# Reciprocal roots as a power on GpSimd, and late additions moved behind a row scaling

## The chip, the cores and the metric

The kernel runs on one core of a Trainium2 chip. A core has five engines that work side by side, each in the order of its own queue: TensorE (PE) multiplies matrices, VectorE (DVE) and ScalarE (ACT) do elementwise work, GpSimd (POOL) does elementwise work on SBUF alone, and SyncE (SP) issues DMAs. The metric is the device time of one execution in microseconds (us), lower is better. Before the change it is 1952.07 us, the median of 3 runs (1950.82 to 1953.63).

## The reference

One layer of a streaming encoder on 1024 tokens with 1024 features, float32: a feed-forward part, an attention, and another feed-forward part, each behind a root-mean-square norm.

```python
def rms_norm(x, gain):
    y = xf * lax.rsqrt(jnp.mean(xf * xf, axis=-1, keepdims=True) + NORM_EPS)
    return y * gain

x = x + 0.5 * swiglu(rms_norm(x, n1), wi1, wo1)      # 1024 -> 2 x 2816 -> 1024
x = x + stick_breaking_attention(rms_norm(x, mix_norm), w_qkv, q_gain, k_gain, w_o)
x = x + 0.5 * swiglu(rms_norm(x, n2), wi2, wo2)
```

In the attention there are 16 heads of 64 features. q and k of every token and head go through the same norm over their 64 features. With z = q k / 8 the weight of an earlier token s for token t is sigmoid(z[t,s]) times the product of sigmoid(-z[t,j]) over the tokens j between them; the output is the weighted sum of v, times w_o.

## The kernel before, in words

Tokens are kept in 8 blocks of 128 rows, in the order 4, 5, 6, 7, 0, 1, 2, 3 (ORDER). Every product is made of three float32r products of high and low parts (mm3, L275): a value is split into a rounded copy made by ScalarE and the rest made by VectorE or GpSimd (split, L183).

The feed-forward parts work with seven half-size products instead of eight. In ffn_out (L509) these are run in the order of SEVEN: 5, 1, 4, 3, 7, 2, 6. Each adds its four banks of PSUM, named ma or mb, to one or two quarters of x (result, L570, the additions are L573 on VectorE). For all but one product this follows at once. Product 2 is the exception: its banks, mb, are read later, during product 6, which works in ma. finish_late (L536) makes these late additions in two parts, and LATE (L88) says for each part behind which operand chunk of product 6 its additions are issued (the low part of that chunk on VectorE) and for which of the four row blocks: part 0 behind chunk 2 for blocks 0 and 1, part 1 behind chunk 4 for blocks 2 and 3. Each block takes two additions, since product 2 goes to two quarters. Part 0 is called ahead of chunk 0's products, part 1 behind them.

The norm in front of the attention is woven into the end of that first feed-forward part, by the function named at (L666), which ffn_out calls at given points. Rows 4 and 5 are normed when product 7 is done. For rows 6 and 7, squares and roots (rates, L223) are made during product 2 and the scaling (L245) during product 6, behind chunk 4's low part; they are transposed (turned, L252, the transposes are L257) into the four mb banks at product 6's first block. Rows 0 to 3 get their squares in two halves, ScalarE's L221; the second half and the rest of the norm follow each block's result. Row 0 is transposed at product 6's last block, the others among the first matmuls of the attention, where row 3's norm is also made.

rsqrt (L189) is the reciprocal root: a scaling to the mean plus epsilon (a), a first guess from the bits of the number (L198), and three Newton steps of three VectorE instructions each (L200 to L202). For a norm of rows it starts from sums added on VectorE (L230) and all is on VectorE. For q and k the a is made by ScalarE (L197), and y lies in a free corner (room) of the PSUM bank that the projection used.

The attention works head pair by head pair, eight pairs. For each, qkv (L750) projects the 8 row blocks to q, k, v in two halves of four blocks, half 1 first, in PSUM banks bq. finish (L771) empties a bank: squares, copies of q and k and v's high part on ScalarE (L774, L775, L778), v's low part (L779) and the sums of squares (L780) on VectorE. After the fourth block of a half it makes the root of 128x16 sums of squares, copies k's part of it to r (L786), multiplies k's rows by r on GpSimd (L790, L793) and puts q's part times 0.125 and -0.125 into f (L797), which scales the sigmoids (L856). Scores (L852) are followed per tile by two sigmoids on ScalarE (L856), a running product as a scan on VectorE (L858) and a product on GpSimd (L865, behind a memset, L863); these weights are transposed by TensorE (L887), split (th on ScalarE, tl on VectorE, L185 and L186) and multiplied with v (L905, bank bo).

What runs when is laid out in a plan: each pair has four parts a, b, c, d with lengths, the steps of all functions get due times in them, and they are issued in the order of these times; each engine's own queue is then ordered at build time by priority and expected readiness, which issue_after constrains. Pair p + 1's projections are spread over pair p, so that one root falls in part c and one in d or a.

Weights of a pair come in four pieces by DMA and are split by ScalarE (L742) and GpSimd (L745). weights_of (L720) can hold a split back: it writes a small instruction (L740) into the tile that the split will write, whose input is some other value, so that the split can't start before that value is there. For the pairs after the second, the first two pieces are held by r on VectorE (for the high part) and by k's product on GpSimd (for the low part). For the first pair, the last two pieces are held by the transposed row 7 (last_x, on GpSimd), and the first two by nothing.

After the first feed-forward part x goes to DRAM (L673) in SP's queue; the stores of rows 0 to 3 are kept in a list, stores, and issued behind the first pair's weight loads.

Of the kernel before, what the change touches and what calls it, by code (L numbers as in the profile page):

```python
# [17 lines left out]
P = 128  # L18
T = 1024
D = 1024  # L20
# [64 lines left out]

ON_POOL_H = {2: (1,), 6: (1, 3, 5)}

LATE = ((2, (0, 1)), (4, (2, 3)))  # L88

W_OF = {  # L90
    1: ((0, 0), (1, 1), "add"), 2: ((0, 0),), 3: ((0, 1), (1, 1), "subtract"), 4: ((1, 0), (0, 0), "subtract"),
# [17 lines left out]
def macaron_kernel(ctx, tc, x, g1, w1_in, w1_out, gm, w_qkv, gq, gk, w_o, g2, w2_in, w2_out, out):  # L109
# [64 lines left out]
    make_identity(nc, ident)  # L174
    xh = cpool.tile([P, KD, T], F32R, name="xh")
    xl = cpool.tile([P, KD, T], F32R, name="xl")
    above = cpool.tile([P, 104], F32, name="above")
    pool_e.memset(below, 0.0)
    pool_e.memset(above, 0.0)
    x_keep = [dram.tile([T, D], F32, name=f"x_keep{i}") for i in range(2)]  # L180
    o_keep = [dram.tile([NP * P, T], F32, name=f"o_keep{n}") for n in "hl"]

# [3 lines left out]
            (engine or dve).tensor_tensor(lo, raw, hi.bitcast(F32), op=ALU.subtract).ins,  # L186
        )

    def rsqrt(pool, ss, inv_n, y=None):  # L189

        shape = list(ss.shape)
        a, u = (pool.tile(shape, F32, name=f"rs_{n}", bufs=2 if y is None else 1) for n in "au")
        if y is None:
            y = pool.tile(shape, F32, name="rs_y")
            dve.tensor_scalar(a, ss, inv_n, EPS, op0=ALU.mult, op1=ALU.add)
        else:
            act.activation(a, ss, AF.Copy, scale=inv_n, bias=EPS)  # L197
        dve.tensor_scalar(y.bitcast(I32), a.bitcast(I32), -0.5, -550020641.0, op0=ALU.mult, op1=ALU.add)  # L198
        for _ in range(3):
            dve.scalar_tensor_tensor(out=u, in0=y, scalar=0.5, in1=a, op0=ALU.mult, op1=ALU.mult)  # L200
            dve.tensor_tensor(u, u, y, op=ALU.mult)
            dve.scalar_tensor_tensor(out=y, in0=u, scalar=1.5, in1=y, op0=ALU.subtract, op1=ALU.mult)  # L202
        return y

    def load_gain(pl, g):
# [14 lines left out]
                junk = pl["hs"].tile([P, NHALF], F32, name="hs", bufs=1)  # L220
                act.activation(junk, row(tb, h), AF.Square, accum_out=ss[:, i, h : h + 1])  # L221

    def rates(pl, row, tbs, ss=None):  # L223

        n = len(tbs)
        if ss is None:
            ss = pl["xs"].tile([P, n, 2], F32, name="ss")
            squares(pl, row, tbs, ss)
        st = pl["xs"].tile([P, n], F32, name="st")
        dve.tensor_tensor(st, ss[:, :, 0], ss[:, :, 1], op=ALU.add)  # L230
        return rsqrt(pl["xs"], st, 1.0 / D)

    def norm(pl, row, tbs, gain, ss=None, r=None, behind=None):

        if r is None:
            r = rates(pl, row, tbs, ss)
        turns = []  # L240
        for i, tb in enumerate(tbs):
            xs = pl["xs"].tile([P, D], F32, name="xs")
            with tc.issue_after(behind) if behind is not None else nullcontext():
                for h in range(2):
                    dve.scalar_tensor_tensor(  # L245
                        out=xs[:, HALVES[h]], in0=row(tb, h), scalar=r[:, i : i + 1], in1=gain[:, HALVES[h]],
                        op0=ALU.mult, op1=ALU.mult,
                    )
            turns.append(partial(turned, xs, tb))
        return turns  # L250
# [258 lines left out]
    def ffn_out(pl, w_out, keep, x_from, ahead, at):  # L509
# [37 lines left out]
        for m, tag, fresh, goes in SEVEN:  # L547
            last = m == SEVEN[-1][0]
            late = m == SEVEN[-2][0]
            if fresh:  # L550
                open_banks[tag] = [bank(tag) for _ in range(4)]
            bs = open_banks[tag]
            ops = [operands(m, c) for c in range(len(CHUNKS))]
            for (th, h), _ in goes:
                if (th, h) not in loaded:
                    load(th, h)
                    loaded.add((th, h))

            def add(ts, cs):
                for c in cs:  # L560
                    (wh, wl), (hh, hl), _ = ops[c]
                    for i, q in enumerate(CHUNKS[c]):
                        for t in ts:
                            s = slice(t * P, (t + 1) * P)
                            mm3(
                                bs[t], [((hh[:, i, s], hl[:, i, s]), (wh[:, i], wl[:, i]))],
                                fresh and q == 0, q == NQ - 1, not fresh,
                            )

            def result(t, bs=bs, goes=goes):  # L570
                for (th, h), sign in goes:
                    xc = x_sb[h][:, 4 * (1 - th) + t, :]
                    dve.scalar_tensor_tensor(out=xc, in0=bs[t], scalar=0.5 * sign, in1=xc, op0=ALU.mult, op1=ALU.add)  # L573

            if last:
                late_result(ops, 0)
            n = len(CHUNKS) - BY_BLOCK if last else len(CHUNKS)
            for c in range(n):
                add(range(4), [c])
                at(x_sb, m, c, ops)  # L580
                if last and c == 0:
                    late_result(ops, 1)
            for t in range(4):
                add([t], range(n, len(CHUNKS)))
                if not late:
# [33 lines left out]
    with pools(*RAWS) as pr:  # L619
# [41 lines left out]
        with banks("ps2"), pools(*SECOND) as pl:  # L661
            lay_banks()
            gain_m = load_gain(pn, gm)
            half = pn["xs"].tile([P, 4, 2], F32, name="half", bufs=1)

            def at(x_sb, m, where, ops):  # L666
                def row(tb, h):
                    return x_sb[h][:, tb, :]

                def store(tbs, hs):  # L670
                    for tb in tbs:
                        for h in hs:
                            sp.dma_start(x_keep[0][rows(tb), HALVES[h]], row(tb, h))  # L673

                def turn_rows(bk, n):
                    for _ in range(n):
                        pending.pop(0)(bk)

                if (m, where) == (7, "end"):
                    pending.extend(norm(pn, row, (4, 5), gain_m))  # L680
                    store((4, 5, 6, 7), (0, 1))
                elif (m, where) == (2, 2):
                    turn_rows("ma", 2)
                elif (m, where) == (2, 3):
                    late.append(rates(pn, row, (6, 7)))
                elif (m, where) == (6, 0):

                    pending.extend(norm(pn, row, (6, 7), gain_m, r=late.pop(), behind=ops[4][2][3]))
                elif m == 2 and str(where).startswith("end"):
                    ts = slice(*((0, 2), (2, 4))[int(where[-1])])  # L690
                    squares(pn, row, range(4)[ts], half[:, ts], (0,))
                elif m == 6 and str(where).startswith("block"):
                    t = int(where[-1])
                    turn_rows("mb", (2, 0, 0, 1)[t])
                    squares(pn, row, (t,), half[:, t : t + 1], (1,))
                    last_norm = lambda: pending.extend(norm(pn, row, (t,), gain_m, half[:, t : t + 1]))
                    if t < 3:
                        last_norm()
                    else:
                        late.append(last_norm)  # L700
                    stores.append(partial(store, (t,), (0, 1)))

            ffn_out(pl | pr, w1_out, keep, x, ops, at)

# [5 lines left out]
    with ExitStack() as stack:  # L710
# [39 lines left out]
        def qkv(p, state):  # L750
# [8 lines left out]
            def step(half, i, ks):  # L759
                if i == 0 and ks.start == 0:  # L760
                    start(half)
                if ks.start == 0:
                    state["ps"] = bank("bq")
                room, ps = state["ps"][:, 3 * P :], state["ps"][:, : 3 * P]
                wh, wl = state["wq"]
                t = rows(half * 4 + i)
                mm3(ps, [((xh[:, k, t], xl[:, k, t]), (wh[k], wl[k])) for k in ks], ks.start == 0, ks.stop == KD)
                if ks.stop == KD:
                    finish(half, i, ps, room)

            def finish(half, i, ps, room):  # L771
# [8 lines left out]
                dve.tensor_reduce(out=ssq[:, i, :], in_=sq, axis=AX.X, op=ALU.add)  # L780
                if i < 3:
                    return
                y = rsqrt(pl["sq"], ssq.rearrange("p a b -> p (a b)"), 1.0 / DH, room[:, :16])
                y = y.rearrange("p (a b) -> p a b", b=4)
                r = state["r"] = pl["sq"].tile([P, 4, 4], F32, name="r", bufs=1)
                dve.tensor_scalar(r[:, :, 0:2], y[:, :, 2:4], 1.0, None, op0=ALU.mult)  # L786
# [7 lines left out]

                f = state["f", half] = pl["sq"].tile([P, 2, 4, 2], F32, name=f"f{half}")
                for n, c in enumerate((0.125, -0.125)):
                    dve.tensor_scalar(f[:, n], y[:, :, 0:2], c, None, op0=ALU.mult)  # L797

            return [
                partial(step, half, i, ks)  # L800
# [138 lines left out]
        steps = qkv(0, states[0])  # L939

        last_x = ((pool_e, 0, lambda: xl[:, KD - 1, T - P : T - P + 1].bitcast(F32)),)
        for f in weights_of(0, states[0], ((), last_x)):
            f()
        with tc.issue_after(states[0]["loaded"]):
            for f in stores:
# [212 lines left out]
```

## Time and profile before

| | |
|---|---|
| median of 3 runs | 1952.07 us (1950.82 to 1953.63) |
| the profiled execution, its own time | 1951.8 us |
| its span, first to last instruction | 1950.0 us |
| granted TensorE clock, mean | 0.999 |
| TensorE busy | 1910.0 us, 98% |
| VectorE busy | 1267.2 us, 65% |
| GpSimd busy | 1092.4 us, 56% |
| ScalarE busy | 986.9 us, 51% |
| first feed-forward part | from 0 to about 672 us |
| attention, with its output projection | to about 1316 us |

How to read the lines below. A group gives line, engine, operation, output and inputs with their shape and count, then busy time and mean length of one in ns, then the idle time of the engine just before it and what ended that. A wait line gives who waited for whom, and then the total, the count and the longest wait in us. A timeline line gives start and length in us, then the instruction; the brackets at its end tell how long the engine had been idle before it and what it waited for. Several instructions of one kind in a row are merged, xN, and the length is then that of all. A window line gives the window, its length, and the busy time of PE, PEld, DVE, ACT and POOL with their counts, the granted clock, the DMA share and GB/s.

### The profile page before, as it was taken

To read this page: it belongs to the slowest core of one execution; us is meant where nothing else is said; L and a number is where in the kernel's file an instruction comes from. 1 tells how busy PE (TensorE), PEld (TensorE's weight loads), DVE (VectorE), ACT (ScalarE), POOL (GpSimd) and SP (SyncE) were. 2 spreads that over 40 slices of the span, in tenths; PEclk is the share of its full clock that TensorE was granted. 3 is DMA by queue.
4 is the path that set the end of the run, shared out by engine and by line. 5 is a ranking of instruction groups with operands and counts; after the bars stand their busy time and mean duration, and the time that the engine had idled before them with its cause. 6 is when DMAs were issued, how large, how long until landed. Compare 5 with 4: busy or idle time off the path is not lost.

```text
span 1950.0 us, 27326 instructions
## 1 busy us (share of the span) xinstructions
PE 1910.0 (98%) x9656; PEld 1639.0 (84%) x9656; DVE 1267.2 (65%) x1834; ACT 986.9 (51%) x1802; POOL 1092.4 (56%) x963
## 2 busy tenths in 40 slices
PE   7999999999999999999999999999999999999998
PEld 7978888888888898888989897789888888888887
DVE  7855545635876867878787878475645545548644
ACT  6533443344334457777787877344433343343332
POOL 3667667655545636656655664113666666655554
PEclk9999999999999999999999999999999999999999
DMA  6223223338896411011011134521323232369973
GB/s 211 82 92 125 98 97 104 118 114 277 322 344 229 139 34 43 32 43 49 28 39 45 60 114 167 179 70 43 129 87 121 98 103 88 129 211 339 337 267 134
DMA packets 168505, 260.26 MB, mean 133 GB/s; under 512 B 11568, under 2 KB 81200, under 8 KB 168368
## 3 DMA queue, kind: packets, MB, share of 16 engines
q1 hardware_dynamic: 168368, 258.52, 38.8%
q8 instruction: 75, 1.23, 0.3%
q14 instruction: 62, 0.51, 0.1%
HBM read 198.18 MB, written 60.29 MB: 133 GB/s over the span
## 4 chain that ended last, share of the span: by engine, by line
PE 85%; DVE 8%; ACT 3%; issue 2%; POOL 2%; DMA 1%; DVEq 0%; POOLq 0%; ACTq 0%
PE ka L282 6%; PE ka L284 6%; PE ka L283 6%; PE kc L284 4%; PE kc L282 4%; PE kc L283 4%; PE kb L284 4%; PE kb L282 4%; PE kb L283 4%; PE ma L283 4%; PE ma L284 4%; PE ma L282 4%; PE bq L282 4%; PE bq L283 4%; PE bq L284 4%; PE bo L905 3%
## 5 line engine op out<-in xcount | busy, mean ns | idle before, releaser
L186 POOL TENSOR_TENSOR u<-sf,u 128x512 fp32r<-128x512 f32 x160 | 226.1, 1415 | 150.9 <-ACT u L185 147.0
L186 POOL TENSOR_TENSOR rp<-raw,rp 128x1024 fp32r<-128x1024 f32 x84 | 208.9, 2491 | 179.1 <-ACT rp L185 168.3
L186 POOL TENSOR_TENSOR u<-raw,u 128x512 fp32r<-128x512 f32 x136 | 196.2, 1448 | 164.2 <-ACT u L185 162.9
L185 ACT ACTIVATE u<-sf 128x512 fp32r<-128x512 f32 x160 | 100.7, 630 | 214.8 <-PE kb L283 86.8
L865 POOL TENSOR_TENSOR w<-w,om 128x512 f32<-128x512 f32 (+4 forms) x128 | 141.1, 1106 | 114.6 <-DVE om L858 88.3
L401 DVE TENSOR_TENSOR h<-h 128x512 f32<-128x512 f32 x110 | 135.4, 1234 | 85.9 <-POOL h L505 85.1
L282 PE MATMUL bq<-wqh,xh 128*128 128x384 f32 x512 | 174.8, 341 | 2.1 <-DVE vst L779 2.1
L284 PE MATMUL bq<-wqh,xl 128*128 128x384 f32 x512 | 172.2, 336 | 0.0
L283 PE MATMUL bq<-wql,xh 128*128 128x384 f32 x512 | 172.1, 336 | 0.0
L185 ACT ACTIVATE rp<-rh 128x1024 fp32r<-128x1024 f32 (+1 forms) x78 | 76.4, 984 | 188.0 <-issue 57.5
L282 PE MATMUL ka<-xh,u 128*128 128x512 f32 (+1 forms) x448 | 162.2, 362 | 1.5 <-ACT s L453 1.5
L283 PE MATMUL ka<-xl,u 128*128 128x512 f32 (+1 forms) x448 | 162.1, 362 | 0.0
L284 PE MATMUL ka<-xh,u 128*128 128x512 f32 (+1 forms) x448 | 161.9, 361 | 0.0
L527 DVE TENSOR_TENSOR raw<-raw 128x1024 f32<-128x1024 f32 (+1 forms) x60 | 97.6, 1629 | 99.0 <-DMA raw<-w_out 89.1
L185 ACT ACTIVATE u<-raw 128x512 fp32r<-128x512 f32 x136 | 84.9, 631 | 148.9 <-PE ka L283 101.2
L282 PE MATMUL ma<-rp 128*128 128x512 f32 x352 | 137.5, 390 | 0.0
L283 PE MATMUL ma<-rp 128*128 128x512 f32 x352 | 137.2, 390 | 0.0
L284 PE MATMUL ma<-rp 128*128 128x512 f32 x352 | 137.2, 390 | 0.0
L856 ACT ACTIVATE w<-bz,f 128x512 f32<-128x512 f32 (+2 forms) x192 | 112.5, 586 | 41.5 <-PE bz L852 38.9
L505 POOL TENSOR_TENSOR h<-h,g 128x512 f32<-128x512 f32 x80 | 113.0, 1412 | 35.1 <-DVE h L457 33.3
L430 DVE TENSOR_TENSOR sf<-raw 128x512 f32<-128x512 f32 x80 | 81.2, 1015 | 78.0 <-POOL u L186 77.9
L186 DVE TENSOR_TENSOR rp<-rh,rp 128x1024 fp32r<-128x1024 f32 (+1 forms) x70 | 106.2, 1535 | 22.6 <-ACT rp L185 19.7
(272 smaller groups left out, 5557.8 us busy)
## 6 DMA issues: line engine op xcount, KB each, us to landing
raw<-w_out SPq DMA_DIRECT2D x120, 512.0 KB, 5.4
raw<-w_in SPq DMA_DIRECT2D x88, 512.0 KB, 3.6
k<-h SPq DMA_DIRECT2D x154, 256.0 KB, 2.1
rh<-k SPq DMA_DIRECT2D x64, 512.0 KB, 5.8
raw_qkv<-w_qkv SPq DMA_DIRECT2D x64, 192.0 KB, 2.9
x_keep<-x SPq DMA_DIRECT2D x32, 256.0 KB, 3.7
x<-x_keep SPq DMA_DIRECT2D x32, 256.0 KB, 5.2
raw<-w_out SPq DMA_DIRECT2D x24, 256.0 KB, 4.7
```

The lines of the kernel that those rows point to most:

```text
L185: act.activation(hi, raw, AF.Copy).ins,
L186: (engine or dve).tensor_tensor(lo, raw, hi.bitcast(F32), op=ALU.subtract).ins,
L282: pe.matmul(dst, ah, bh, start=start and i == 0, stop=False, skip_group_check=onto)
L283: pe.matmul(dst, ah, bl, start=False, stop=False, skip_group_check=onto)
L284: pe.matmul(dst, al, bh, start=False, stop=stop and i == n - 1, skip_group_check=onto)
L401: dve.tensor_tensor(src, hb[of[0]], hb[of[1]], op=getattr(ALU, of[2]))
L430: dve.tensor_tensor(f[n], x, y, op=op)
L505: pool_e.tensor_tensor(h, h, gs[k], op=ALU.mult)
L527: dve.tensor_tensor(w[0], w[0], w[1], op=getattr(ALU, W_OF[m][2]))
L856: act.activation(to, z, AF.Sigmoid, scale=state["f", half][:, sign, tb % 4, hd : hd + 1])
L865: pool_e.tensor_tensor(wt[:, c1 : c0 + n], wt[:, c1 : c0 + n], om[:, c1 - 1 : c0 + n - 1], op=ALU.mult)
L905: pe.matmul(ot[:, :n], vv, t[:, c : c + n], start=start, stop=stop)
```

## The change

- The constant tile power holds -0.5 in each partition (a memset on GpSimd); the tile above shrinks from 104 to 96 columns.
- A new function root makes the reciprocal root in two GpSimd instructions: the scaling to a, and a to the power -0.5 as a tensor_tensor with power spread over the columns.
- In the attention, finish uses root in place of rsqrt. r is no longer a copy but a view of y, which has two buffers. The two f are made on GpSimd. Nothing of the root is on VectorE or ScalarE any more, and none of it in PSUM.
- The norm in front of the attention, with pooled=True, adds its two sums of squares on GpSimd and uses root. The other two norms keep rsqrt on VectorE.
- Both parts of the late additions are issued behind chunk 4 of product 6; they are called behind chunk 0 and chunk 1, so behind the call that scales rows 6 and 7.
- The first pair's first two weight pieces get a holding instruction on GpSimd, in the low part's tile, that reads row block 0 of x's first half, which late addition makes. For this the stores carry row along.

```diff
-LATE = ((2, (0, 1)), (4, (2, 3)))
+LATE = ((4, (0, 1)), (4, (2, 3)))
...
+    power = cpool.tile([P, 1], F32, name="power")
...
+    pool_e.memset(power, -0.5)
...
+    def root(pool, ss, inv_n, bufs):
+
+        n = ss.shape[-1]
+        a, y = (pool.tile([P, n], F32, name=f"rs_{i}", bufs=b) for i, b in zip("ay", bufs))
+        pool_e.tensor_scalar(a, ss, inv_n, EPS, op0=ALU.mult, op1=ALU.add)
+        pool_e.tensor_tensor(y, a, power.to_broadcast([P, n]), op=ALU.pow)
+        return y
...
-        dve.tensor_tensor(st, ss[:, :, 0], ss[:, :, 1], op=ALU.add)
-        return rsqrt(pl["xs"], st, 1.0 / D)
+        (pool_e if pooled else dve).tensor_tensor(st, ss[:, :, 0], ss[:, :, 1], op=ALU.add)
+        return root(pl["xs"], st, 1.0 / D, (4, 2)) if pooled else rsqrt(pl["xs"], st, 1.0 / D)
...
-            if last:
-                late_result(ops, 0)
             n = len(CHUNKS) - BY_BLOCK if last else len(CHUNKS)
             for c in range(n):
                 add(range(4), [c])
                 at(x_sb, m, c, ops)
-                if last and c == 0:
-                    late_result(ops, 1)
+                if last and c < 2:
+                    late_result(ops, c)
...
-                y = rsqrt(pl["sq"], ssq.rearrange("p a b -> p (a b)"), 1.0 / DH, room[:, :16])
-                y = y.rearrange("p (a b) -> p a b", b=4)
-                r = state["r"] = pl["sq"].tile([P, 4, 4], F32, name="r", bufs=1)
-                dve.tensor_scalar(r[:, :, 0:2], y[:, :, 2:4], 1.0, None, op0=ALU.mult)
+                y = root(pl["sq"], ssq.rearrange("p a b -> p (a b)"), 1.0 / DH, (1, 2)).rearrange("p (a b) -> p a b", b=4)
+                r = state["r"] = y[:, :, 2:4]
...
-                    dve.tensor_scalar(f[:, n], y[:, :, 0:2], c, None, op0=ALU.mult)
+                    pool_e.tensor_scalar(f[:, n], y[:, :, 0:2], c, None, op0=ALU.mult)
...
-        for f in weights_of(0, states[0], ((), last_x)):
+        added = ((pool_e, 1, lambda: stores[0].args[0](0, 0)[:, 0:1]),)
+        for f in weights_of(0, states[0], (added, last_x)):
```

The calls norm(pn, ...) and rates(pn, ...) of the norm in front of the attention get pooled=True.

More of the change, by code (lines that the diff above doesn't have):

```diff
@@ L176, in macaron_kernel @@
     xl = cpool.tile([P, KD, T], F32R, name="xl")
-    above = cpool.tile([P, 104], F32, name="above")
+    above = cpool.tile([P, 96], F32, name="above")
+    power = cpool.tile([P, 1], F32, name="power")
     pool_e.memset(below, 0.0)
     pool_e.memset(above, 0.0)
+    pool_e.memset(power, -0.5)
     x_keep = [dram.tile([T, D], F32, name=f"x_keep{i}") for i in range(2)]
@@ L187, in split, with rsqrt @@
         )
[L189 to L197, printed above, removed]
+    def rsqrt(pool, ss, inv_n):
+        a, u, y = (pool.tile(list(ss.shape), F32, name=f"rs_{n}") for n in "auy")
+        dve.tensor_scalar(a, ss, inv_n, EPS, op0=ALU.mult, op1=ALU.add)
         dve.tensor_scalar(y.bitcast(I32), a.bitcast(I32), -0.5, -550020641.0, op0=ALU.mult, op1=ALU.add)
@@ L221, in squares, with rates @@
                 act.activation(junk, row(tb, h), AF.Square, accum_out=ss[:, i, h : h + 1])
-    def rates(pl, row, tbs, ss=None):
+    def rates(pl, row, tbs, ss=None, pooled=False):
         n = len(tbs)
@@ L229, in rates, with norm @@
         st = pl["xs"].tile([P, n], F32, name="st")
-        dve.tensor_tensor(st, ss[:, :, 0], ss[:, :, 1], op=ALU.add)
-        return rsqrt(pl["xs"], st, 1.0 / D)
-    def norm(pl, row, tbs, gain, ss=None, r=None, behind=None):
+        (pool_e if pooled else dve).tensor_tensor(st, ss[:, :, 0], ss[:, :, 1], op=ALU.add)
+        return root(pl["xs"], st, 1.0 / D, (4, 2)) if pooled else rsqrt(pl["xs"], st, 1.0 / D)
+    def norm(pl, row, tbs, gain, ss=None, r=None, behind=None, pooled=False):
         if r is None:
-            r = rates(pl, row, tbs, ss)
+            r = rates(pl, row, tbs, ss, pooled)
         turns = []
@@ L668, in row, with store @@
                     return x_sb[h][:, tb, :]
-                def store(tbs, hs):
+                def store(row, tbs, hs):
                     for tb in tbs:
@@ L679, in at @@
                 if (m, where) == (7, "end"):
-                    pending.extend(norm(pn, row, (4, 5), gain_m))
-                    store((4, 5, 6, 7), (0, 1))
+                    pending.extend(norm(pn, row, (4, 5), gain_m, pooled=True))
+                    store(row, (4, 5, 6, 7), (0, 1))
                 elif (m, where) == (2, 2):
@@ L684, in at @@
                 elif (m, where) == (2, 3):
-                    late.append(rates(pn, row, (6, 7)))
+                    late.append(rates(pn, row, (6, 7), pooled=True))
                 elif (m, where) == (6, 0):
@@ L695, in at @@
                     squares(pn, row, (t,), half[:, t : t + 1], (1,))
-                    last_norm = lambda: pending.extend(norm(pn, row, (t,), gain_m, half[:, t : t + 1]))
+                    last_norm = lambda: pending.extend(norm(pn, row, (t,), gain_m, half[:, t : t + 1], pooled=True))
                     if t < 3:
@@ L700, in at @@
                         late.append(last_norm)
-                    stores.append(partial(store, (t,), (0, 1)))
+                    stores.append(partial(store, row, (t,), (0, 1)))
             ffn_out(pl | pr, w1_out, keep, x, ops, at)
@@ L763, in step @@
                     state["ps"] = bank("bq")
-                room, ps = state["ps"][:, 3 * P :], state["ps"][:, : 3 * P]
+                ps = state["ps"][:, : 3 * P]
                 wh, wl = state["wq"]
@@ L768, in step, with finish @@
                 if ks.stop == KD:
-                    finish(half, i, ps, room)
-            def finish(half, i, ps, room):
+                    finish(half, i, ps)
+            def finish(half, i, ps):
                 qk, ssq, vst = state["qk", half], state["ssq"], state["v"]
```

## Prediction

> **What bounds the kernel now.** I read the page's busy times first, then the list of TensorE's waits, then the groups by line, and last the timeline engine by engine at the two places the change touches.
>
> ```profile
> span 1950.0 us, 27326 instructions
> ...
> PE 1910.0 (98%) x9656; PEld 1639.0 (84%) x9656; DVE 1267.2 (65%) x1834; ACT 986.9 (51%) x1802; POOL 1092.4 (56%) x963
> ```
>
> TensorE is busy for 1910.0 of 1950.0 us, and the change leaves it the same matmuls. So it can give back only what lies in TensorE's waits; VectorE's busy time is no measure. The waits, with total, count and longest:
>
> ```profile
> PE kb L257 <- DVE xs L245: 11.8, 4, 9.4
> PE bo L905 <- DVE tl L186: 7.5, 15, 0.9
> PE bt L887 <- POOL w L863: 4.6, 8, 0.6
> PE mb L257 <- DVE x L573: 2.2, 2, 1.9
> PE bq L282 <- DVE vst L779: 2.1, 1, 2.1
> ...
> PE bz L852 <- DVE w L858: 1.4, 7, 0.4
> ...
> PE bz L852 <- DVE rs_u L201: 0.4, 1, 0.4
> PE bz L810 <- POOL qk L790: 0.4, 1, 0.4
> ```
>
> The first (11.8) is the first layer's norm, which the change does not touch. The mb and bq waits lie between the first feed-forward part and the attention, the others in the attention. Within reach are then 7.5 + 2.2 + 2.1 + 1.4 + 0.4 + 0.4 = 14 us at most, 0.7% of the span. The bt wait (4.6) hangs on a sigmoid, scan, product chain without any root in it; it stays. One head pair in the steady state shows the same picture, here as busy times of PE, PEld, DVE, ACT, POOL:
>
> ```profile
> 806.00:872.00 66.00, 64.07 (x387) 58.86 (x385) 52.82 (x102) 51.52 (x112) 37.97 (x57) 1.00 0.13 41
> ```
>
> TensorE has 1.9 us idle in 66; GpSimd has 28 us free, VectorE 13.
>
> **The change part by part.** *The attention's root* (16 times, two per pair).
>
> ```profile
> L202 DVE SCALAR_TENSOR_TENSOR bq<-rs_u,bq 128x16 f32<-128x16 f32 x48 | 8.4, 176 | 1.2
> L200 DVE SCALAR_TENSOR_TENSOR rs_u<-bq,rs_a 128x16 f32<-128x16 f32 x48 | 8.1, 168 | 1.1
> L201 DVE TENSOR_TENSOR rs_u<-rs_u,bq 128x16 f32<-128x16 f32 x48 | 7.5, 157 | 0.6
> ...
> L740 DVE TENSOR_TENSOR wqh<-r 128x2 fp32r<-128x2 f32 x12 | 5.5, 500 | 0.0
> ...
> L797 DVE TENSOR_SCALAR f<-bq 128x8 f32<-128x8 f32 x32 | 3.7, 155 | 0.2 <-issue 0.2
> L198 DVE TENSOR_SCALAR bq<-rs_a 128x16 int32<-128x16 int32 x16 | 2.7, 168 | 0.3 <-ACT rs_a L197 0.3
> L786 DVE TENSOR_SCALAR r<-bq 128x8 f32<-128x8 f32 x16 | 2.6, 163 | 0.4
> ```
>
> Out of VectorE's queue go, per root, 168 + 3 x (168 + 157 + 176) = 1.67 us of steps, 0.16 for r and 0.31 for the two f: 2.1 us, 34 in all, and one small ScalarE instruction. GpSimd gets four instructions: the scaling a, the power y, two f. Its price per instruction follows from two sizes of one line:
>
> ```profile
> L865 POOL TENSOR_TENSOR w<-w,om 128x255 f32<-128x255 f32 x16 | 11.8, 740 | 1.1 <-DVE om L858 1.1
> ...
> L865 POOL TENSOR_TENSOR w<-w,om 128x127 f32<-128x127 f32 x16 | 7.4, 465 | 1.1 <-DVE om L858 0.3
> ```
>
> (740 - 465) / 128 = 2.15 ns a column over 0.19 us fixed: 0.23 us for a (16 columns), 0.2 for each f. No row shows a power. Its floor is 0.23, one ordinary pass. A ceiling is nine ordinary passes, each with its fixed cost, as many as the steps it replaces: 9 x 0.23 = 2.1. I take one fixed cost and nine passes of columns, 0.19 + 9 x 16 x 0.00215 = 0.5 us, since it is one instruction. Then a root occupies GpSimd for 0.23 + 0.5 + 0.4 = 1.1 us, 18 us in all. Does GpSimd have room where they fall? Around one root:
>
> ```profile
> 812.57 0.41 DVE L780 TENSOR_REDUCE ssq<-sq 128x4 f32<-128x256 f32 x1
> ...
> 818.24 0.15 DVE L201 TENSOR_TENSOR rs_u<-rs_u,bq 128x16 f32<-128x16 f32 x1
> ...
> 818.86 0.93 DVE L740 TENSOR_TENSOR wqh<-r 128x2 fp32r<-128x2 f32 x2
> 819.71 0.68 DVE L186 TENSOR_TENSOR tl<-bt,th 128x512 fp32r<-128x512 f32 x1
> ```
> ```profile
> 815.28 1.01 POOL L865 TENSOR_TENSOR w<-w,om 128x383 f32<-128x383 f32 x1 [1.37 <-DVE rs_u L201]
> 818.40 1.29 POOL L865 TENSOR_TENSOR w<-w,om 128x512 f32<-128x512 f32 x1 [2.11 <-DVE rs_u L201]
> ...
> 848.98 1.30 POOL L865 TENSOR_TENSOR w<-w 128x511 f32<-128x511 f32 x1 [1.73 <-DVE rs_u L201]
> ...
> 851.65 1.05 POOL L790 TENSOR_TENSOR qk<-qk,r 128x512 f32<-128x512 f32 x1 [1.34 <-DVE r L786]
> ```
>
> The sums of squares are ready at 813.0, and GpSimd idles 1.37 + 2.11 = 3.48 us before its product of 818.40; the pair's second root has 1.73 + 1.34. So a root of 1.1 us is hidden by this idle time, and the cover ends at a power of 3.48 - 0.23 - 0.4 = 2.85 us. r comes earlier: today its first reader, L740, starts 5.9 us after the reduction; 0.73 us on GpSimd, before or behind its product of 815.28, makes that 2 to 4.
>
> Against moving it speaks GpSimd's own rate: its 1.29 us at 818.40 are for 128x512, which VectorE's tl of 819.71 does in 0.68. The Trainium skill, GPSIMD Engine Reference, section When to use GPSIMD, puts it as a rule: ordinary elementwise work belongs on VectorE, GpSimd being about 2x slower for two inputs. These two rows agree; no run here shows it for a power. By the rule the sum would be that of the last rival below, not mine.
>
> What it gives back: at 818.24 VectorE still does L201, L202, r and two f, then the two copies of r into the weights' tile (L740), 0.93 us together although ones as small take 0.16 (L201), because GpSimd's product of 818.40 runs. Only then comes the tl of 819.71 on which TensorE waits. The same wait stands in six pairs, first and last:
>
> ```profile
> 754.43 0.50 PE L905 MATMUL bo<-tl,vst 128*128 128x512 f32 x1 [0.72 <-DVE tl L186]
> ...
> 1084.90 0.50 PE L905 MATMUL bo<-tl,vst 128*128 128x512 f32 x1 [0.73 <-DVE tl L186]
> ```
>
> Six of these are 4.4 us. All goes if r is early enough that L740 passes before GpSimd's product; nothing if L740 stays beside it. I take 2.7. The nine smaller bo waits (7.5 - 4.4 = 3.1) and the seven bz waits behind w (1.4) are 4.5 together. Some follow a root that fills VectorE's queue, some a scan that came late from ScalarE: I take half, 2.2 (0 to 2.9). The two of 0.4, in the last pair, name the steps and the products behind r themselves: 0.8.
>
> New waits: L740 on VectorE now waits for GpSimd; behind it are the tl and the scans, and TensorE for them. The new GpSimd instructions also hold up VectorE's instructions that read SBUF twice, up to 0.5 us each. I charge 1.0 (0 to 3).
>
> *The norm's root and the order in front of the attention.*
>
> ```profile
> 618.83 2.74 DVE L245 SCALAR_TENSOR_TENSOR xs<-x,rs_y,gain 128x512 f32<-128x512 f32 x4
> ...
> 651.14 6.02 DVE L245 SCALAR_TENSOR_TENSOR xs<-x,rs_y,gain 128x512 f32<-128x512 f32 x4
> 657.08 2.47 DVE L573 SCALAR_TENSOR_TENSOR x<-mb,x 128x512 f32<-128x512 f32 x4
> ...
> 683.51 0.28 DVE L779 TENSOR_TENSOR vst<-bq,vst 128x128 fp32r<-128x128 f32 x1
> ```
> ```profile
> 652.45 5.57 POOL L745 TENSOR_TENSOR wql<-raw_qkv,wqh 128x384 fp32r<-128x384 f32 x4
> ...
> 677.46 1.69 POOL L740 TENSOR_TENSOR wqh<-qk 128x2 fp32r<-128x2 f32 x4 [9.51 <-ACT qk L775]
> ```
> ```profile
> 658.41 0.92 PE L257 MATMUL mb<-ident,xs 128*128 128x128 f32 x4 [1.90 <-DVE x L573]
> ...
> 683.84 0.45 PE L282 MATMUL bq<-wqh,xh 128*128 128x384 f32 x1 [2.11 <-DVE vst L779]
> ```
> ```profile
> 677.26 0.28 ACT L778 ACTIVATE vst<-bq 128x128 fp32r<-128x128 f32 x1
> ```
>
> ScalarE has evacuated its part of the bank at 677.5, but VectorE reaches its L779 only at 683.51, behind the roots of rows 2 and 3: TensorE waits 2.11. With these roots on GpSimd, which idles 9.51 us up to 677.46, VectorE is free in time: -2.1. VectorE's scaling now waits for GpSimd's power, with L573 and L779 queued behind it; the 9.51 us cover that.
>
> Scaling rows 6 and 7 takes 6.02 us beside GpSimd's weight split of 652.45 where four such instructions took 2.74 without it. The new GpSimd instruction that reads row 0 keeps the split behind the first late addition. So the scaling ends 0 to 3.28 us earlier; but now all eight late additions (2 x 2.47) stand behind it instead of four, and the transposes need the banks they free. VectorE's sum of work is the same, so the last bank comes free up to 3.28 us earlier and the wait of 2.2 shrinks by 0 to 2.2: I take -1.1, and +0.5 as the bad end for the first transposes, whose banks are free today. Queued behind the waiting GpSimd instruction are the splits and row 0's root; TensorE wants those weights only after the last block of the feed-forward part. No DMA moves on SP's queue: the stores only carry their row with them. The tiles' sizes and the one memset cost nothing: they lie at the start, beside the loads.
>
> Sum: -2.1 - 1.1 - 2.7 - 2.2 - 0.8 + 1.0 = -7.9 us. The profiled execution took 1951.8 us, 1.8 around its span, and the median of the runs is 1952.1, 0.3 more. 1951.8 - 7.9 = 1943.9, or 1944.2 as a median. All good ends together: -2.1 - 2.2 - 4.4 - 2.9 - 0.8 = -12.4, 1939.7.
>
> **The rivals.** *The waits only change their name.* L740 still meets GpSimd's product, and the small waits are scans that come from ScalarE anyway. Then only the stage before the attention gives, -3.2: 1948.9. For it: L740's mean of 0.50. Against it: r comes 2 to 4 us sooner.
>
> *Slower: the power is dear.* GpSimd works in order; past 2.85 us of power every product behind it is late, and the transposes behind that. At 4 us: 14 roots in the seven steady pairs x 1.15 = 16.1, less 3.2: +12.9, 1965. For it: no row shows a power. Against it: two times the nine-pass ceiling would be needed.
>
> *GpSimd needs twice VectorE's time for the root as well*, as it does for the product of 1.29 against 0.68. Twice 1.67 is 3.3 us of power, 0.45 past the cover, at each of 14 roots: 14 x 0.45 - 3.2 = +3.1, 1955.2. Against it: the power is one instruction, and most of the 1.67 us are the fixed cost of ten. The Trainium skill's rule above would give this.
>
> **How the numbers follow.** Forecast 0.55 (own range 1940 to 1948), names only 0.20, dear power 0.15, twice 0.10. Range 1940 to 1956: it leaves out the dear power and the tails. A measurement of this kernel tells about 0.2%, 3.9 us. Faster by more: 0.60, nearly all of the forecast and some of the second. Same: 0.22, most of the second and of the last. Slower: 0.18.
>
> **What would show it.** A power on GpSimd under 2.85 us; no 2.1 us wait at the bq bank; rows 6 and 7 scaled in 3 to 4 us; the 0.73 waits at bo mostly gone, the bt waits of 0.6 still there. It is wrong if GpSimd's power appears as the releaser of VectorE's waits, or if pairs still take 66 us.

## The result and the profile after

The changed kernel takes 1969.17 us (median of 5 runs, 1968.21 to 1973.42), beside 1952.07 (1950.82 to 1953.63) before: a ratio of 1.0092, 95% interval 1.0077 to 1.0107. It is 17 us slower where 8 us faster were forecast. The profiled execution of after is the longest of its five, 1973.42 us with a span of 1971.6, so sums made against it are some 4 us larger than those of the medians.

The page of after, its span and its busy times (the columns as before):

```profile
span 1971.6 us, 27141 instructions
...
PE 1916.4 (97%) x9656; PEld 1643.6 (83%) x9656; DVE 1233.9 (63%) x1554; ACT 983.6 (50%) x1786; POOL 1158.2 (59%) x1048
```

VectorE's busy time fell by 33.3 us. That it comes near the forecast's 34 is chance: the 34 was for the attention's root, and with the attention alone changed (a run below) it falls by 18.5. GpSimd's rose by 65.8, and by 56.3 with the attention alone, where 18 were forecast for the attention. The groups of GpSimd say why. These are the roots' two instructions and the two f:

```profile
L207 POOL TENSOR_TENSOR rs_y<-rs_a,power 128x16 f32<-128x16 f32 x16 | 46.8, 2924 | 1.2
...
L798 POOL TENSOR_SCALAR f<-rs_y 128x8 f32<-128x8 f32 x32 | 7.0, 237 | 0.0
...
L206 POOL TENSOR_SCALAR rs_a<-ssq 128x16 f32<-128x16 f32 x16 | 3.3, 204 | 5.2 <-DVE ssq L783 3.5 <-PE bt L262 1.0
...
L207 POOL TENSOR_TENSOR rs_y<-rs_a,power 128x1 f32<-128x1 f32 x4 | 2.2, 546 | 0.3
```

The scaling (0.20) and f (0.24) cost what an ordinary pass costs. The power takes 2.92 us for 16 columns and 0.55 for one: (2924 - 546) / 15 = 159 ns a column, over 0.39 us fixed. It is an expensive operation for each value, not one ordinary pass. TensorE's waits in after:

```profile
PE bt L888 <- POOL w L864: 17.9, 16, 3.8
PE kb L262 <- DVE xs L250: 11.2, 4, 9.1
PE bo L906 <- ACT th L187: 9.1, 6, 1.5
PE bo L906 <- DVE tl L188: 4.5, 14, 0.9
...
PE mb L262 <- DVE x L578: 1.1, 2, 0.5
```

The bq wait of 2.1 is gone and mb lost 1.1. But bt has grown from 4.6 to 17.9, and a wait of 9.1 for ScalarE's th is new. All rows of the two lists make 50.9 against 34.3 us, 16.6 more; TensorE's busy time is 6.4 more for the same matmuls. Together 23.0, about the 21.6 by which the span grew.

**The new wait of 1.52 us at bo**, once in each of six pairs. GpSimd, VectorE, ScalarE and TensorE around one of them, in the timeline of after:

```profile
885.76 0.20 POOL L206 TENSOR_SCALAR rs_a<-ssq 128x16 f32<-128x16 f32 x1
886.05 2.92 POOL L207 TENSOR_TENSOR rs_y<-rs_a,power 128x16 f32<-128x16 f32 x1
```
```profile
885.92 0.95 DVE L859 TENSOR_TENSOR_SCAN om<-bz,first 128x384 f32<-128x384 f32 x1
889.01 1.11 DVE L743 TENSOR_TENSOR wqh<-rs_y 128x2 fp32r<-128x2 f32 x2 [2.14 <-POOL rs_y L207]
890.57 0.69 DVE L188 TENSOR_TENSOR tl<-bt,th 128x512 fp32r<-128x512 f32 x1 [0.45 <-ACT th L187]
```
```profile
889.20 0.84 ACT L745 ACTIVATE wqh<-raw_qkv 128x768 fp32r<-128x768 f32 x1 [3.81 <-DVE wqh L743]
889.95 0.58 ACT L187 ACTIVATE th<-bt 128x512 fp32r<-128x512 f32 x1
```
```profile
890.59 0.50 PE L906 MATMUL bo<-th,vst 128*128 128x512 f32 x1 [1.52 <-ACT th L187]
```

Read it from the end. TensorE waits for th. th stands in ScalarE's queue behind the split L745 of the weights of a pair that comes two later. That split is held by VectorE's L743, which waits for y, and y is the power. ScalarE idles for 3.81 us with th behind the waiting instruction. So a holding instruction that carries nothing urgent puts the power into the path.

**The bt waits.** The second root of the pair, on GpSimd, with the scan whose product comes late, and the transposition that waits:

```profile
850.15 2.92 POOL L207 TENSOR_TENSOR rs_y<-rs_a,power 128x16 f32<-128x16 f32 x1
853.16 1.05 POOL L791 TENSOR_TENSOR qk<-qk,rs_y 128x512 f32<-128x512 f32 x1
854.18 0.44 POOL L798 TENSOR_SCALAR f<-rs_y 128x8 f32<-128x8 f32 x2
854.61 1.32 POOL L794 TENSOR_TENSOR qk<-qk,rs_y 128x256 f32<-128x256 f32 x2
855.89 0.90 POOL L866 TENSOR_TENSOR w<-w 128x127 f32<-128x127 f32 x1
```
```profile
850.67 0.42 DVE L859 TENSOR_TENSOR_SCAN w<-bz,first 128x128 f32<-128x128 f32 x1
```
```profile
856.85 0.33 PE L888 MATMUL bt<-ident,w 128*128 128x128 f32 x1 [1.05 <-POOL w L864]
```

The scan is done at 851.1, its product starts at 855.89, 4.8 us later: the power, k's products and f stand between in GpSimd's queue. The list names L864, a small memset, as releaser; by the timeline it is the queue behind the power. A wait of 1.05 to 1.07 us stands there in five pairs, one of 0.60 in a sixth. In the first and the last pair this wait is 3.81 and 3.47 us, and TensorE's clock falls behind it. The windows behind the first (the third figure from the end is the granted clock):

```profile
716.00:720.00 4.00, 1.93 (x7) 1.41 (x8) 0.00 (x0) 0.53 (x1) 3.92 (x10) 0.61 0.00 0
720.00:724.00 4.00, 4.00 (x17) 3.81 (x16) 3.34 (x5) 3.26 (x9) 1.97 (x4) 0.54 0.00 0
```

In these 8 us the clock is little more than half. The wait of 3.81 agrees with the Trainium skill, TensorE: Matmul & The Clock Gate, Part 1, by which an idle window of about 3.4 us takes the clock to half and about as long a busy one restores it. But the clock fell behind shorter waits as well: behind the last of the six waits of 1.5 named above, at 1094.98 (0.83 over 1090 to 1100), and in the profiled execution of before behind the mb wait of 1.90 (0.87 and 0.79 over 655 to 665). In the run below with the attention alone the same mb wait left it at 1.00. So no length of wait at which the clock falls comes out of these traces.

### The profile page after: what moved, and what is told of

It reads as the page before. It is cut to its first block, busy times and chain, and to the rows that moved or that the text cites. A ratio compares the mean times of both kernels' runs of the same rounds, so it can differ in the third digit from the quotient of the medians.

```text
span 1971.6 us, 27141 instructions
## 1 busy us (share of the span) xinstructions
PE 1916.4 (97%) x9656; PEld 1643.6 (83%) x9656; DVE 1233.9 (63%) x1554; ACT 983.6 (50%) x1786; POOL 1158.2 (59%) x1048
## 4 chain that ended last, share of the span: by engine, by line
PE 84%; POOL 5%; DVE 5%; ACT 4%; issue 2%; DMA 1%; SPq 0%; ACTq 0%; DVEq 0%; POOLq 0%
PE ka L287 6%; PE ka L288 6%; PE ka L289 6%; PE kc L288 4%; PE kc L287 4%; PE kc L289 4%; PE kb L288 4%; PE kb L287 4%; PE kb L289 4%; PE bq L288 4%; PE bq L287 4%; PE bq L289 4%; PE ma L289 3%; PE ma L288 3%; PE ma L287 3%; PE mb L289 3%
## 5 line engine op out<-in xcount | busy, mean ns | idle before, releaser
L532 DVE TENSOR_TENSOR raw<-raw 128x1024 f32<-128x1024 f32 (+1 forms) x60 | 89.7, 1498 | 102.7 <-DMA raw<-w_out 86.4
L857 ACT ACTIVATE w<-bz,f 128x512 f32<-128x512 f32 (+1 forms) x192 | 112.4, 586 | 44.1 <-PE bz L853 41.6
L188 DVE TENSOR_TENSOR rp<-rh,rp 128x1024 fp32r<-128x1024 f32 (+1 forms) x70 | 117.4, 1694 | 22.6 <-ACT rp L187 19.9
```

Source lines behind the costliest of these rows:

```text
L532: dve.tensor_tensor(w[0], w[0], w[1], op=getattr(ALU, W_OF[m][2]))
L857: act.activation(to, z, AF.Sigmoid, scale=state["f", half][:, sign, tb % 4, hd : hd + 1])
```

## The experiments

The theory after reading these traces: the whole loss is the power's length on GpSimd, by two ways, the products behind it in GpSimd's queue (bt) and the hold that reads r (bo). The rivals: the new order of the queues loses the time, whatever the power takes; the loss comes from the part in front of the attention; the hold has no share in it.

**The same queues, a cheap instruction in the power's place.** It computes something else: the rates are a times -0.5 instead of a to the power -0.5.

```diff
-        pool_e.tensor_tensor(y, a, power.to_broadcast([P, n]), op=ALU.pow)
+        pool_e.tensor_tensor(y, a, power.to_broadcast([P, n]), op=ALU.mult)
```

> The power is replaced by a product with the same operands (so the rates are wrong), and every engine's queue stays as it is. Theory A, the power's length: with 0.2 us in place of 2.92 the waits of 1.5 at bo and 1.05 at bt go, and the time falls to what the prediction had without this term, 1942 to 1948 us. Rival B, the place: VectorE and ScalarE now stand behind GpSimd, which makes the products with r before the attention's own products whatever the power takes; then 2.4 us of products per root stay in the way and the time stays above 1958 us.

Measured: 1946.21 us, ratio 0.9973 (0.9961 to 0.9985). Its waits, and the place where before waited 0.73:

```profile
PE bt L888 <- POOL w L864: 6.6, 10, 1.1
PE bo L906 <- DVE tl L188: 5.4, 15, 1.3
```
```profile
748.97 0.50 PE L906 MATMUL bo<-tl,vst 128*128 128x512 f32 x1 [0.22 <-DVE tl L188]
```

Every engine has its instructions in the same order as in after, only the one instruction is short, and 23 us are gone:

```profile
L207 POOL TENSOR_TENSOR rs_y<-rs_a,power 128x16 f32<-128x16 f32 x16 | 3.5, 216 | 1.2
```

The length of the power is the cause; the rival of the queues' order falls. With a cheap power the change would give 5 us (1951.24 for before beside this run).

**The norm in front of the attention alone** (the attention's root and f back on VectorE) and **the attention alone** (everything in front of it as before).

```diff
...
-                y = root(pl["sq"], ssq.rearrange("p a b -> p (a b)"), 1.0 / DH, (1, 2)).rearrange("p (a b) -> p a b", b=4)
-                r = state["r"] = y[:, :, 2:4]
+                y = rsqrt(pl["sq"], ssq.rearrange("p a b -> p (a b)"), 1.0 / DH, room[:, :16])
+                y = y.rearrange("p (a b) -> p a b", b=4)
+                r = state["r"] = pl["sq"].tile([P, 4, 4], F32, name="r", bufs=1)
+                dve.tensor_scalar(r[:, :, 0:2], y[:, :, 2:4], 1.0, None, op0=ALU.mult)
...
```

> The norm in front of the attention, the late additions and the hold by row 0 as in the changed kernel, the attention's root back on VectorE. Theory A: the norm's part gives the 4.5 us by which the fourth sum of squares came earlier (692.9 to 688.4), and the attention costs nothing: 1946 to 1949 us. Rival C, the norm's part only moves the wait into the first pair: 1951 to 1953 us.

```diff
-LATE = ((4, (0, 1)), (4, (2, 3)))
+LATE = ((2, (0, 1)), (4, (2, 3)))
...
-        return root(pl["xs"], st, 1.0 / D, (4, 2)) if pooled else rsqrt(pl["xs"], st, 1.0 / D)
+        return rsqrt(pl["xs"], st, 1.0 / D)
...
-        for f in weights_of(0, states[0], (added, last_x)):
+        for f in weights_of(0, states[0], ((), last_x)):
```

> The attention's root on GpSimd, all ahead of it as before the change. Theory A: all of the loss and none of the gain, 17 + 4.5 us over the kernel before: 1971 to 1976 us. Rival C: 1968 to 1971 us.

Measured: 1946.32 (ratio 0.9973, 0.9963 to 0.9983) and 1972.11 (1.0103, 1.0088 to 1.0118). The waits of the second:

```profile
PE bt L890 <- POOL w L866: 18.0, 16, 3.8
PE bo L908 <- ACT th L187: 9.1, 6, 1.5
...
PE bq L287 <- DVE vst L784: 2.4, 1, 2.4
```

The part in front of the attention gains 5 us and the attention's part loses about 21. The bt and bo waits of after are all there, and the bq wait has stayed with the norm's roots on VectorE.

**What of the part in front carries its gain.** The kernel with the norm alone, and in it the late additions and the first pair's weights back to the order of before: only the norm's roots lie on GpSimd.

```diff
-LATE = ((4, (0, 1)), (4, (2, 3)))
+LATE = ((2, (0, 1)), (4, (2, 3)))
...
-        for f in weights_of(0, states[0], (added, last_x)):
+        for f in weights_of(0, states[0], ((), last_x)):
```

> Of the norm's part only the roots on GpSimd; the late additions and the first pair's weight split as before the change. Theory A: the wait of 2.1 us at the bq bank goes, the waits of 2.2 at mb and the lower clock behind them (0.87 and 0.79 over 10 us) stay: 1948 to 1950 us. Rival: the roots alone carry all of the gain: 1946 to 1947 us.

Measured: 1946.51 (0.9975, 0.9965 to 0.9985), the same time as with the new order. The list of waits has no bq and still `mb`:

```profile
PE mb L267 <- DVE x L583: 2.2, 2, 1.7
```

So the roots carry the gain alone. The new order shortens the mb wait (2.2 here, 1.1 in after), and no run shows a gain in time from it.

**No hold by r.** The first way out of the bo wait, by leaving that hold out:

```diff
-                    ((dve, 0, lambda s=nxt: s["r"][:, 0, 0:1]), (pool_e, 1, lambda s=nxt: s["qk", 1][:, 0, 4, 0:1])),
+                    ((pool_e, 1, lambda s=nxt: s["qk", 1][:, 0, 4, 0:1]),),
```

> The changed kernel without VectorE's small instruction that reads r and holds back the weight split; the hold by k's product on GpSimd stays. Theory D: in part c the loss goes over this instruction (VectorE idle 2.14 us before it, ScalarE's split and th behind it), six pairs by some 1.7 us: 1957 to 1962 us. Rival E: GpSimd's own queue holds the pair anyway, since the product of 383 columns follows the root and its products: 1966 to 1970 us.

Measured: 1978.25 (1.0135, 1.0118 to 1.0152), slower still, and outside what either side expected. Nothing now keeps the split behind its place, and the queues came out in another order. ScalarE and TensorE:

```profile
782.09 0.84 ACT L745 ACTIVATE wqh<-raw_qkv 128x768 fp32r<-128x768 f32 x1 [1.06 <-DMA raw_qkv<-w_qkv]
```
```profile
784.08 0.45 PE L906 MATMUL bo<-th,vst 128*128 128x384 f32 x1 [3.00 <-ACT th L187]
```

The splits stand ahead of their DMA, and th behind them. The run says what the hold is for, and nothing on what it costs when y is late.

**The hold by another value.** v's low part of the last block of the first half is made on VectorE shortly before the root, and doesn't come from GpSimd; all queues keep the order of after.

```diff
-                    ((dve, 0, lambda s=nxt: s["r"][:, 0, 0:1]), (pool_e, 1, lambda s=nxt: s["qk", 1][:, 0, 4, 0:1])),
+                    ((dve, 0, lambda s=nxt: s["v"][:, 7, 1, 0:1].bitcast(F32)), (pool_e, 1, lambda s=nxt: s["qk", 1][:, 0, 4, 0:1])),
```

> The changed kernel, every engine's queue in the same order; VectorE's small instruction in front of the weight split reads v's last block, which VectorE itself has written, and no longer r. Theory D: in part c the loss goes over this instruction, six pairs by 1.5 to 1.75 us: 1958 to 1961 us. Rival E: GpSimd's own queue (the product of 383 columns behind the root and its products) makes TensorE wait as long at the next transposes: 1966 to 1970 us.

Measured: 1955.92 (1.0019, 1.0010 to 1.0029). Its waits, and the hold on VectorE:

```profile
PE bt L888 <- POOL w L864: 17.9, 16, 3.8
...
PE bo L906 <- DVE tl L188: 3.0, 8, 0.9
```
```profile
815.46 0.21 DVE L743 TENSOR_TENSOR wqh<-vst 128x2 fp32r<-128x2 f32 x2
```

The th wait is gone, the bt wait has not moved: two separate ways. One value that a small instruction reads is worth 1969.2 - 1955.9 = 13.3 us by the medians, and 12.3 when each is taken against before in its own runs (1952.07 and 1951.14). That is more than the six waits of 1.52 (9.1); the rest is smaller waits behind tl (4.5 to 3.0) and TensorE's busy time (1908.3 us here, 1916.4 in after). The two profiled executions differ by more, 19.1, as the one of after was the longest of its five and TensorE's clock was lower in it more often. The two instructions of the hold now take 0.21 instead of 1.11 us: beside them GpSimd is in its power (2.92 us from 814.73), and no longer in a product.

**The root in two halves**, eight columns behind two blocks each, so that half of it is done early.

```diff
...
+                if i % 2 == 0:
+                    return
+                cols = slice(8 * (i // 2), 8 * (i // 2) + 8)
+                ra, ry = state["a"][:, cols], state["y"][:, cols]
...
+                pool_e.tensor_tensor(ry, ra, power.to_broadcast([P, 8]), op=ALU.pow)
...
```

> The changed kernel with each attention root made in two pieces of 8 columns, the first after two of the four blocks. GpSimd spends no less in all, but only the second piece, some 1.5 us instead of 2.92, follows the last sum. Theory A, the delay behind the last sum is what costs: the waits in parts c and a and in the first and last pair shrink by about 1.4 us each, 1969 - 7 x 2.5 to 1969 - 7 x 1.5: 1952 to 1960 us. Rival, GpSimd's total work is what costs: 1967 to 1971 us.

Measured: 1971.23 (1.0097, 1.0081 to 1.0112); the 1952 to 1960 were missed. The power of a half, the waits, and one of the new ones:

```profile
820.75 1.63 POOL L791 TENSOR_TENSOR rs_y<-rs_a,power 128x8 f32<-128x8 f32 x1
```
```profile
PE bz L819 <- DVE om L867: 13.6, 6, 2.3
...
PE bt L896 <- POOL w L872: 9.5, 10, 2.5
```

2.92 - 1.63 = 1.29 us is what the last piece is shorter, and the longest bt wait fell from 3.81 to 2.54, by 1.27: the length passes one to one to TensorE there. In the steady pairs the th waits and the bt waits of 1.05 are gone, and six waits of 2.27 have come, at k's transposition. TensorE's queue has the order of after, but the hold now reads the first piece of y, and the build put it ahead of a scan on VectorE, behind which it stood before. GpSimd, VectorE and TensorE at one of them:

```profile
802.14 1.66 POOL L791 TENSOR_TENSOR rs_y<-rs_a,power 128x8 f32<-128x8 f32 x1
```
```profile
803.84 0.23 DVE L743 TENSOR_TENSOR wqh<-rs_y 128x2 fp32r<-128x2 f32 x2 [2.33 <-POOL w L872]
803.99 0.95 DVE L867 TENSOR_TENSOR_SCAN om<-bz,first 128x384 f32<-128x384 f32 x1
```
```profile
804.99 0.66 PE L819 MATMUL bz<-ident,qk 128*128 128x128 f32 x4 [2.27 <-DVE om L867]
```

The list names a memset again, by the timeline it is the power. The hold waits for it, the scan stands behind the hold, and k's transposition needs the bank that the scan reads. So the same hold brought the power back into the path at another place. What the halves would give without that, this run doesn't show.

**The power twice**, a second time behind the first, for the roots of 16 columns.

```diff
-        pool_e.tensor_tensor(y, a, power.to_broadcast([P, n]), op=ALU.pow)
+        for _ in range(2 if n == 16 else 1):
+            pool_e.tensor_tensor(y, a, power.to_broadcast([P, n]), op=ALU.pow)
```

> The changed kernel with each power of 16 columns made a second time behind the first, into the same tile. By the theory that the power's length on GpSimd is what costs, each of the 14 roots of the seven steady pairs delays what stands behind it by another 2.9 us: where a root already waits on the path (part c and part a) TensorE loses all of it, 14 x 2.9 = 41 us, and waits of 6 us lower TensorE's clock behind them as the first pair's 3.8 did: 2005 to 2025. By the rival that the loss comes from what the queues' new order does and not from the length, the second power falls into GpSimd's idle time and the time stays within 10 us of the changed kernel's 1969.

Measured: 2026.64 (1.0382, 1.0363 to 1.0400), 57 us above after, a little past the upper end. Its waits, two bo waits one pair apart, and the clock behind the first:

```profile
PE bt L889 <- POOL w L865: 33.0, 15, 6.4
PE bo L907 <- ACT th L187: 26.9, 6, 4.5
```
```profile
836.48 0.79 PE L907 MATMUL bo<-th,vst 128*128 128x512 f32 x1 [4.49 <-ACT th L187]
913.58 0.80 PE L907 MATMUL bo<-th,vst 128*128 128x512 f32 x1 [4.48 <-ACT th L187]
```
```profile
836.00:840.00 4.00, 3.52 (x11) 2.91 (x12) 2.41 (x4) 3.37 (x7) 4.00 (x10) 0.51 0.00 0
```

The bo wait grew from 1.52 to 4.49, by 2.97, the whole second power (2.91). Now it is long enough that the clock falls to 0.51 in these pairs too: the matmul of 0.50 takes 0.79. That makes the step larger than 14 times the power: in the profiled executions TensorE's waits grew by 37 us and its busy time by 16.

**Two tries at the waits of 0.73 of before**, on the kernel with the norm alone, where the root is VectorE's. First the hold as an instruction with one input, to see if two reads of SBUF make it slow beside GpSimd's product:

```diff
-                    engine.tensor_tensor((h_, l_)[to][:, ks, 0], there, there, op=ALU.mult)
+                    if engine is dve:
+                        engine.tensor_scalar((h_, l_)[to][:, ks, 0], there, 1.0, None, op0=ALU.mult)
+                    else:
+                        engine.tensor_tensor((h_, l_)[to][:, ks, 0], there, there, op=ALU.mult)
```

> The kernel with the norm's part alone (1946.3 us), VectorE's small instruction made with one SBUF input instead of two. Theory F: its 0.93 us for two come from standing beside GpSimd's product, which one input does not; the wait of 0.73 at bo goes in six pairs: 1942 to 1944 us. Rival: the tl behind it waits for ScalarE's th anyway: 1945 to 1947 us.

Measured: 1945.55 (0.9968, 0.9955 to 0.9981), the 0.74 waits unchanged. The group of the hold:

```profile
L749 DVE TENSOR_SCALAR wqh<-r 128x2 fp32r<-128x2 f32 x12 | 5.5, 502 | 0.0
```

502 ns with one input, 500 with two: that theory fell. By the Trainium skill, SBUF — State Buffer, section Who interferes with whom, a VectorE instruction with one SBUF input meets GpSimd only in a mode that uses both ports, which tensor_scalar can enter. Whether this one did, no run here shows.

Then the hold by v in the same kernel, so that it stands in front of the root's steps:

> The attention's root is VectorE's as before, the norm's root on GpSimd, and VectorE's holding instruction reads v's low part instead of r. If the six waits of 0.73 to 0.74 us at bo come because the holding instruction stands behind the root on VectorE and in front of tl, beside GpSimd's product, they go: six times 0.5 to 0.7 = 3 to 4 us off the 1946.3 of the kernel with the norm's root alone, 1942 to 1944, pairs of about 65.5 us instead of 66.0. The rival is that the root's steps themselves hold up tl, whoever the holding instruction waits for: then the waits stay at 0.7 and the time at 1945 to 1947.

Measured: 1941.25 (0.9947, 0.9934 to 0.9961), better than both kernels. Its waits, and the place of the 0.73 in two pairs:

```profile
PE bo L913 <- DVE tl L188: 3.0, 8, 0.9
```
```profile
749.73 0.50 PE L913 MATMUL bo<-tl,vst 128*128 128x512 f32 x1
...
814.89 0.50 PE L913 MATMUL bo<-tl,vst 128*128 128x512 f32 x1
```

No wait stands at that place any more, and the pair takes 814.89 - 749.73 = 65.2 us. It was the hold's place in the queue, beside GpSimd's product and in front of tl. The same edit in after (1955.92) and here (1941.25) also shows what the attention's power still costs with the hold moved: 14.7 us by the medians. In the two lists of waits only the bt rows differ by much (17.9 against 4.7 for the longest).

## Why the prediction was wrong

- **The power's price failed.** The step was "one fixed cost and nine passes of columns, 0.5 us", with nine whole passes, 2.1, as the ceiling. It takes 2.92, nearly 6 times the value taken and 0.8 above the ceiling. The bound counted VectorE's steps; nothing in the trace tied the power to them. An operation without a row has no ceiling from rows of other operations. Neither "twice VectorE's time" (3.3) nor the rule named beside it is a law for it, but that figure was the nearest.
- **The cover failed too, and without it the right price would not have given the right time.** With 2.92 in its own formula, (2.92 - 2.85) x 14 - 3.2 gives 1950. The cover of 2.85 added two idle stretches of GpSimd (1.37 and 2.11) that a product of 1.01 separates, and counted only GpSimd. Missing were the instructions that wait for y: k's products of 1.05 and 1.32, which move back behind the power, ahead of the product that TensorE needs (bt, 1.05 in most pairs and 3.81 and 3.47 in the first and the last); and the chain from y over the hold to ScalarE's split and th (bo, 1.52). The prediction names the hold's readers as "the tl and the scans"; th behind ScalarE's split was not followed.
- **"New collisions", +1.0 (0 to 3), is the term of the sum in which this belongs.** By the trace: six times 1.52, five times 1.06 and once 0.60, and 3.81 + 3.47, make 22.3, and 6.4 us of TensorE's busy time, mostly at a lower clock. With the waits that went set against them, the two lists differ by the 16.6 above.
- **The bq wait** of 2.1: right. It goes with the norm's roots alone and stays without them. The roots alone gave 4.6 us by the medians, more than this wait; what the rest is stays open.
- **The late additions**, -1.1: the wait at mb shrank (2.2 to 1.1), and scaling rows 6 and 7 takes 4.79 us, not the 3 to 4 named. Two kernels with and without the new order take the same time, so the term was not seen.
- **The six waits of 0.73**, -2.7: the mechanism was right, where the power is cheap. There they became 0.22, 6 x 0.5 = 3.
- **The nine smaller waits and the last pair**, -2.2 and -0.8: not seen as a gain. With a cheap power bt waits 6.6 (4.6 before) and bo still 5.4; the whole change then gives 5.0 us by the medians of that run (1951.24 before), not 7.9, which is about what the norm's roots give alone.
- **The rival "the power is dear"** named this mechanism, priced it past 2.85 us and put its 1965 nearest to the result, with a chance of 0.15 where the unknown price deserved more. That it came so near is luck: it took a power of 4 us, and with the 2.92 measured the same formula gives the 1950 above.

What stays open: what the late additions' order is worth, which is below what these runs tell; and what the root in halves would give in the steady pairs if the hold kept its place.

## What to carry to other kernels

An operation that no row shows has no upper bound from rows of others; if it stands in an in-order queue, follow every instruction that reads its result, those behind them in each queue too, until one that TensorE waits for. Idle time of an engine is cover only in one piece and only for what nobody waits for. And a small instruction that merely holds something back should read the earliest value that serves: here the choice of that value was worth 12 to 13 us in one kernel and 5 to 6 in another.

## What the runs showed of the hardware

- A power on GpSimd took 0.55, 1.63 and 2.92 us for 1, 8 and 16 columns of 128 partitions, while a product of 16 columns took 0.22. VectorE's ten steps for the same root take 1.67.
- Behind the waits of 3.8 and of 4.5 us shown above TensorE's clock was about half for some 4 us (0.54 and 0.51 in a window), so such a wait cost more than its length. Behind the six waits of 1.5 it stayed at 1.00 five times, and behind a wait of 1.9 it fell in one execution and not in another: these runs show no threshold.
- Two instructions of 128x2 on VectorE took 1.11 us beside a product of GpSimd, and 0.21 beside GpSimd's power.
